# A hybrid mixer with a hierarchical mixture of experts: state products issued together, level differences on VectorE, gates through SBUF, weights staged in two buffers

## The chip, the cores and the metric

The kernel runs on one core of one Trainium2 chip. The metric is the device time of one execution in microseconds (us). The engines are TensorE (PE in the profile, with PEld for its weight loads), VectorE (DVE), ScalarE (ACT), GpSimd (POOL) and SyncE (SP), which issues most DMAs. Each engine works through its own instructions in the order in which they were put into its queue.

## What is computed

The input has 1024 tokens of width 1024. The reference, cut to what matters here:

```python
hq, hf, hi, hg, gq, gk, gv, ga, gg = jnp.split(x @ w_in, split_at, axis=-1)
f = lb + (1 - lb) * sigmoid(hf)
o_h = chunk_gla(hq * 128 ** -0.5, 1 - f, hi, log(f))           # 4 heads, key width 128
o_h = head_rms_norm(o_h, norm_h) * silu(hg)
log_a = log_sigmoid(ga @ w_a2 + b_a) / 16
o_g = chunk_gla(gq * 64 ** -0.5, gk, gv, log_a)                # 4 heads, key width 64
o_g = head_rms_norm(o_g, norm_g) * silu(gg)
h = concatenate([o_h, o_g]) @ w_out
x = layer_norm(ALPHA * x + h)
y = top-2 of 64 experts: (silu(x @ w_gate[e]) * (x @ w_up[e])) @ w_down[e], weighted
out = layer_norm(ALPHA * x + y)

# chunk_gla: with b the running sum of log_g inside a chunk,
#   o[t] = sum over s <= t of (q[t] * exp(b[t] - b[s]) . k[s]) v[s]  +  (q[t] * exp(b[t])) . S
#   S    = g_chunk * S + (k * exp(b_last - b))^T v                  (from chunk to chunk)
```

## The kernel before, in words

The kernel has three stages: the mixer (projections and gated linear attention), the output projection with the first norm and the router, and the experts.

**Projections.** `queue` (lines 265 to 279) is a list of 26 blocks of 128 columns of `w_in`: keys `k0..k5`, queries `q0..q5`, values `v0..v7`, gates `g0..g7`, and the low-rank input `ga`. `block(i)` (line 158) multiplies one such block with all tokens, in two halves of 512 tokens, each 24 matmuls of 128x512 (line 168) into one of two PSUM tiles `pp`; products are made of a rounded part and a rest (`wh` and `wl`, `xh` and `xl`). At its start a block has the next block's weights staged by `weights` (line 142): for each half of the weights SP loads the raw numbers into `wr` (line 154), ScalarE casts them into `wh` (line 155), and VectorE subtracts to get `wl` (line 156). After the last matmul of a half, the block's `evac` takes the result out of `pp`: keys and queries on ScalarE (lines 241 to 246); values by a copy into a tile `vt` (line 208), which TensorE later transposes (line 213) and VectorE copies into `VOA` (line 214); a gate by Silu on ScalarE (line 220) and a multiply into `VOA` on VectorE (line 222).

**Attention.** The loop `for u in range(6)` (line 625) goes through six units: four with one head of key width 128 and two with two heads of width 64. A unit's chunk is 128 tokens, so there are eight chunks. `prepare(u)` forms the log decays `lg` and their running sum `P` (lines 402 to 425). `level(li)` (line 459), for li from 0 to 6, scales keys and queries for the score blocks of size 2^li. For li from 1 on it forms a tile `d`: GpSimd subtracts `P` from a reference position for the first half of each block (line 481), ScalarE takes the exponential (line 482), VectorE multiplies the keys (line 483); GpSimd subtracts again for the second half (line 484), ScalarE takes the exponential (line 485), and VectorE multiplies the queries (line 486). Two buffers of `d` exist. `scores(li)` multiplies keys and queries on TensorE (line 497 and following) and VectorE masks the results into `acc` (lines 448 and 451). `states()` (line 561) multiplies the decayed keys `KLt` with the values for seven chunks (line 566), into two PSUM tiles of one bank each (four chunks and three), and VectorE chains the results: a copy for the first chunk (line 568), then one multiply-add per chunk (line 570) that reads the state before it. `outputs(half)` multiplies states and scores with queries and values (lines 583 and 586), ScalarE sums squares (line 591) and VectorE copies the result into `osb` (line 592). `norm()` (line 594) forms the inverse root of the mean square with thirteen small VectorE steps (lines 82 to 90) and multiplies `osb` (line 600); `turn_o` transposes it back into `VOA` (lines 607 and 608).

**Order.** TensorE's order is written out by hand in `mixer()` (line 613): `fill(n)` issues the next n projection matmuls, and the pieces of attention stand between such fills. Around the states of unit u the order is: the rest of the block, the fourteen instructions of `states()`, `fill(38)`, `outputs(0)` with the first three levels of unit u + 1 issued after it, `fill(38)`, `outputs(1)`, `norm()`, `fill(12)`, and then unit u + 1 with `scores(0)`, levels 3 and 4, `decayed_k`, `fill(26)`, `scores(1)`, `scores(2)`, levels 5 and 6, `fill(26)`, `turn_o(0)` of unit u, and so on. The order on the other engines is made by a scheduler out of the program's order. Where two instructions touch the same PSUM bank of a tile and one of them writes, the later one waits for the earlier one.

**Afterwards.** The output projection (`w_out`, line 899) and the router follow; then the loop over 32 pairs of experts (line 1276), whose weights SP loads in units of 2 MB into eight buffers (`load_unit`, line 758), each load as soon as the buffer's last reader is done.

Of the kernel before, what the change touches and what calls it, by code (L numbers as in the profile page):

```python
# [10 lines left out]
F32 = mybir.dt.float32  # L11
# [10 lines left out]
NT = T // 128  # L22
# [35 lines left out]
def mixer_moe_kernel(ctx: ExitStack, tc: tile.TileContext, x_in, xT_in, wf_in, wv_in, wvg_in, wa2_in,  # L58
# [68 lines left out]

    zt = g2.tile([128, 512], F32, name="vt", bufs=4)[:, 0:256].bitcast(BF)
    V.memset(zt, 0.0)
# [12 lines left out]
    def weights(i, parts=2):  # L142

        if queue[i][0] is None:
            wts[i] = gahl, None
            return
        hi = wst.tile([128, KT, 128], F32R, name="wh")
        lo = wst.tile([128, KT, 128], F32R, name="wl")
        m = KT // parts
        wts[i] = hi, lo  # L150
        for j in range(parts):
            ks = slice(j * m, j * m + m)
            raw = wst.tile([128, m, 128], F32, name="wr", bufs=1)
            nc.sync.dma_start(raw, queue[i][0][:, ks])
            heads.append(S.copy(hi[:, ks], raw))
            V.tensor_tensor(lo[:, ks], raw, hi[:, ks], OP.subtract)  # L156
# [45 lines left out]
    def to_rows(h):  # L202

        def evac(ps, ts):
            if len(late) > 3:
                late.pop(0)[1]()
            vt = g2.tile([128, 512], F32, name="vt", bufs=4)
            S.copy(vt, ps)

            def turn():  # L210
                tp = bank4()
                for i in range(4):
                    PE.transpose(tp[:, i], vt[:, i * 128:(i + 1) * 128], ident)
                V.tensor_copy(VOA[:, ts.start // 128:ts.stop // 128, h], tp)
            late.append((count[0] + 6, turn))
        return evac

    def gated(h):
        def evac(ps, ts):
            S.activation(ps, ps, AF.Silu)  # L220
            o = VOA[:, ts.start // 128:ts.stop // 128, h]
            V.tensor_tensor(o, o, ps.rearrange("p (a b) -> p a b", b=128), OP.mult)  # L222
        return evac
# [209 lines left out]
    def gla(u):  # L433
# [25 lines left out]
        def level(li):  # L459
# [16 lines left out]
            else:  # L476
                nb = T // (2 * h)
                e = g2.tile([128, T], F32, name="d")
                ev = v4(e)
                ref = Pv[:, :, 0, h - 1:h].to_broadcast([128, nb, h])  # L480
                G.tensor_tensor(ev[:, :, 0], ref, Pv[:, :, 0], OP.subtract)  # L481
                S.activation(ev[:, :, 0], ev[:, :, 0], AF.Exp, scale=sc)
                V.tensor_tensor(Kv[:, :, 0], kv[:, :, 0], ev[:, :, 0], OP.mult)
                G.tensor_tensor(ev[:, :, 1], Pv[:, :, 1], ref, OP.subtract)
                S.activation(ev[:, :, 1], ev[:, :, 1], AF.Exp, scale=sc)
# [75 lines left out]
        def states():  # L561
            ups = [bank4() for _ in range(2)]
            for c in range(NT - 1):
                up = ups[c // 4][:, c % 4]
                for hh in range(nh):
                    PE.matmul(up[rows[hh]], dd["KLt"][:, c, rows[hh]], VOA[:, c, h0 + hh], start=True, stop=True)
                if c == 0:
                    V.tensor_copy(St[:, c], up)
# [24 lines left out]

        def norm():

            sq = ssq[0].rearrange("p h c -> p (h c)")
            V.tensor_scalar(sq, sq, 1.0 / 128, None, op0=OP.mult)
            rs = rstd_of(small, sq, nh * NT, "n").rearrange("p (h c) -> p h c", h=nh)
# [3 lines left out]
        def turn_o(hh):  # L602
            gain = cols[:, 10 + h0 + hh:11 + h0 + hh]
            for half in range(2):
                tp = bank4()
                for i in range(4):
# [3 lines left out]
        return SimpleNamespace(level=level, scores=scores, decayed_q=decayed_q, decayed_k=decayed_k, turn_k=turn_k,  # L610
                               states=states, outputs=outputs, norm=norm, turn_o=turn_o, nh=nh, v=f"v{h0 + nh - 1}")

    def mixer():
# [11 lines left out]
        for u in range(6):  # L625
# [3 lines left out]
            un.level(3)  # L629
            un.level(4)  # L630
            un.decayed_k()
            fill(26)
# [43 lines left out]
            old.outputs(1)  # L676
            old.norm()
        fill(34)
# [894 lines left out]
```

## Time and profile before

| what | us |
|---|---|
| median of 2 runs | 1596.03 (1595.31 to 1596.76) |
| profiled execution: its time | 1599.36 |
| profiled execution: its span | 1597.6 |
| TensorE busy | 1461.5 (91% of the span) |
| VectorE busy | 705.7 |
| ScalarE busy | 438.6 |
| GpSimd busy | 388.7 |
| DMA from HBM | 447.58 MB read |

The profile is of one execution. A row of its groups gives line, engine, operation, output and inputs, shapes and count, and after the bar the busy time, the mean of one instruction in ns, and the idle time of the engine just before them with what ended it. In the timeline, the bracket at a row's end is the idle time of the engine before that instruction and its releaser. In a table of windows each engine has its busy time and, in brackets, its instruction count; PEclk is the share of full clock that TensorE was granted. A matmul of 128x512 is shown with 0.39 us, but such matmuls overlap: at full clock one starts about every 0.227 us.

### The profile page before, as it was taken

How to read it: one execution, taken by the hardware profiler on the slowest of the kernel's cores; microseconds unless marked ns; L12 is line 12 of the kernel's file. 1: busy time of each engine (PE TensorE's matmuls, PEld its weight loads, DVE VectorE, ACT ScalarE, POOL GpSimd, SP SyncE). 2: the span in 40 equal slices, each digit the busy share in tenths (PEclk: the TensorE clock that was granted, in tenths of full speed). 3: DMA queues.
4: the chain of work that ended last, by engine and by line, in shares of the span. 5: the costliest groups of instructions: out<-in, count | busy, mean ns of one | idle time of the engine just before them, and what ended most of it. 6: DMA issues, size and time to landing. Idle time of an engine off the chain costs nothing. (4 is left out here: it accounts for less than half of the span.)

```text
span 1597.6 us, 23051 instructions
## 1 busy us (share of the span) xinstructions
PE 1461.5 (91%) x9411; PEld 815.6 (51%) x9411; DVE 705.7 (44%) x1632; ACT 438.6 (27%) x915; POOL 388.7 (24%) x275
## 2 busy tenths in 40 slices
PE   8978989979889999999999999899989999989997
PEld 6766768767678887434333334334333334333342
DVE  6648456272736378333433324323323422422433
ACT  6535445333633243221211211211111111111120
POOL 1434223050600222131312211311311311321212
PEclk9989999988989999999999999999999999999999
DMA  4101001100013834999999999999999999999995
GB/s 167 41 27 35 26 29 35 27 29 28 21 35 124 318 138 175 406 425 426 427 425 426 427 426 426 426 425 426 425 426 427 427 425 425 427 426 426 426 419 221
DMA packets 62606, 449.14 MB, mean 281 GB/s; under 512 B 12320, under 2 KB 20768, under 8 KB 36896
## 3 DMA queue, kind: packets, MB, share of 16 engines
q1 hardware_dynamic: 51184, 430.01, 64.8%
q0 software_dynamic: 9216, 12.61, 2.2%
q10 hardware_dynamic: 2096, 5.01, 0.8%
q8 instruction: 75, 1.23, 0.3%
q14 instruction: 35, 0.29, 0.1%
HBM read 447.58 MB, written 20.97 MB: 293 GB/s over the span
## 5 line engine op out<-in xcount | busy, mean ns | idle before, releaser
L1298 PE MATMUL gu<-w2u,VOA 128*64 128x512 f32 x992 | 340.9, 597 | 20.3 <-DMA w2u<-in_wg_dram 11.4
L1298 PE MATMUL gu<-w1u,VOA 128*64 128x512 f32 x1040 | 344.0, 597 | 15.5 <-DMA w1u<-in_wg_dram 14.2
L1298 PEld LDWEIGHTS gu<-w2u,VOA 128*64 128x64 f32 x992 | 101.9, 137 | 200.1 <-issue 155.9
L1133 ACT ACTIVATE VOA<-tp,cols 128x128 f32<-128x128 f32 x256 | 96.1, 456 | 334.7 <-PE tp L1130 334.4
L1298 PEld LDWEIGHTS gu<-w1u,VOA 128*64 128x64 f32 x1040 | 106.4, 137 | 146.8 <-issue 113.1
L168 PE MATMUL pp<-xh,wh 128*128 128x512 f32 x416 | 173.6, 417 | 7.7 <-DVE VOA L222 4.2
L1341 PE MATMUL yp<-w2u,hT 128*64 128x512 f32 x496 | 170.0, 598 | 11.0 <-DVE hT L1150 11.0
L1341 PE MATMUL yp<-w1u,hT 128*64 128x512 f32 x496 | 168.0, 598 | 11.8 <-DVE hT L1150 11.8
L1120 POOL DMA_INDIRECT out_dram<-VOA,oidx x32 | 32.4, 1011 | 582.1 <-DVE VOA L1180 561.4
L168 PE MATMUL pp<-xl,wh 128*128 128x512 f32 x416 | 172.7, 415 | 0.0
L168 PE MATMUL pp<-xh,wl 128*128 128x512 f32 x416 | 172.6, 415 | 0.0
L1244 DVE SCALAR_TENSOR_TENSOR VOA<-VOA,cp 128x512 f32<-128x512 f32 x62 | 41.6, 682 | 259.5 <-PE cp L1230 250.3
L1157 DVE SCALAR_TENSOR_TENSOR y<-yp,gcol,y 128x512 fp32r<-128x512 f32 x62 | 46.5, 751 | 227.6 <-ACT y L1156 227.4
L481 POOL TENSOR_TENSOR d<-P 128x512 f32<-128x512 f32 x36 | 60.4, 1678 | 181.8 <-DVE P L425 70.6
L168 PEld LDWEIGHTS pp<-xh,wh 128*128 128x128 f32 x416 | 83.8, 201 | 28.3 <-DVE VOA L222 5.3
L1156 ACT ACTIVATE y<-yp,gcol 128x512 fp32r<-128x512 f32 x62 | 42.5, 687 | 187.9 <-PE yp L1341 185.4
L168 PEld LDWEIGHTS pp<-xl,wh 128*128 128x128 f32 x416 | 83.9, 202 | 18.4 <-issue 0.3
L168 PEld LDWEIGHTS pp<-xh,wl 128*128 128x128 f32 x416 | 83.9, 202 | 18.2 <-DVE wl L156 0.2
L1341 PEld LDWEIGHTS yp<-w1u,hT 128*64 128x64 f32 x496 | 48.1, 136 | 76.9 <-issue 60.3
L1304 ACT ACTIVATE sg<-gu 128x512 f32<-128x512 f32 x32 | 19.1, 598 | 247.9 <-PE gu L1298 247.9
L1341 PEld LDWEIGHTS yp<-w2u,hT 128*64 128x64 f32 x496 | 51.1, 136 | 62.0 <-issue 44.2
L1230 PE MATMUL cp<-y,same 128*128 128x512 f32 x316 | 82.1, 405 | 0.0
(313 smaller groups left out, 2096.8 us busy)
## 6 DMA issues: line engine op xcount, KB each, us to landing
w1u<-in_wg_dram SPq DMA_DIRECT2D x30, 2048.0 KB, 26.7
w2u<-in_wg_dram SPq DMA_DIRECT2D x30, 2048.0 KB, 29.0
w2u<-in_wu_dram SPq DMA_DIRECT2D x30, 2048.0 KB, 30.0
w1u<-in_wd_dram SPq DMA_DIRECT2D x30, 2048.0 KB, 28.9
w1u<-in_wu_dram SPq DMA_DIRECT2D x29, 2048.0 KB, 29.3
w2u<-in_wd_dram SPq DMA_DIRECT2D x28, 2048.0 KB, 28.9
wr<-in_wf_dram SPq DMA_DIRECT2D x36, 256.0 KB, 2.7
w1u<-in_wg_dram SPq DMA_DIRECT2D x6, 1024.0 KB, 26.3
```

Of the source, the lines that this page charges most:

```text
L168: PE.matmul(ps, w[:, k], x_[:, k, ts], start=(k == 0 and j == 0), stop=(k == KT - 1 and j == len(terms) - 1))
L481: G.tensor_tensor(ev[:, :, 0], ref, Pv[:, :, 0], OP.subtract)
L1120: return G.indirect_dma_start(out=dst, out_offset=bass.IndirectOffsetOnAxis(ap=idx, axis=0), in_=src, in_offset=None, bounds_check=rows - ...
L1133: S.activation(xt[:, c], tp[:, i], AF.Identity, bias=cols[:, 42 + c:43 + c], scale=cols[:, 34 + c:35 + c])
L1156: S.mul(yh[:, ns], yps[n], gate_col)
L1157: V.scalar_tensor_tensor(yl[:, ns], yps[n], gate_col, yh[:, ns], op0=OP.mult, op1=OP.subtract)
L1230: PE.matmul(cps[n], m, ys[q][:, i, n * 512:(n + 1) * 512], start=(not part and j == 0 and i == 0), stop=(not part and j == len(ms) - 1 and ...
L1244: o = V.scalar_tensor_tensor(xg[:, ns], xg[:, ns], ALPHA, cps[n], op0=OP.mult, op1=OP.add)
L1298: PE.matmul(dst[64 * b:64 * b + 64], xt[:, c, 64 * b:64 * b + 64], utile[6 * p + u + b][:, c], start=(c == 0), stop=(c == KT - 1))
L1304: silu = S.activation(sg, gp, AF.Silu)
L1341: PE.matmul(yps[n][64 * b:64 * b + 64], hT[:, c, 64 * b:64 * b + 64], utile[6 * p + 4 + b][:, c, n * 512:(n + 1) * 512], start=(c == 0), s ...
```

## The change

Seven edits, in the order of the diff. The pool `vt` has three buffers instead of four, and `late` (value halves waiting to be transposed) holds one less before the oldest is turned. `wr` has two buffers instead of one. For the gates of heads 0 to 5, Silu writes into a `vt` tile in SBUF instead of back into `pp`, and the multiply reads that tile. A level forms both halves' differences with one VectorE instruction over 1024 columns (`P` minus reference) instead of two GpSimd instructions over 512, and the first half's exponential takes the opposite sign of scale. `states()` issues the products of all seven chunks and then the chain. `norm()` of a unit is called in the next unit after its level 4, and its first VectorE step is ordered behind that level's last multiply; the last unit's norm is called after the loop.

```diff
-    zt = g2.tile([128, 512], F32, name="vt", bufs=4)[:, 0:256].bitcast(BF)
+    zt = g2.tile([128, 512], F32, name="vt", bufs=3)[:, 0:256].bitcast(BF)
...
-            raw = wst.tile([128, m, 128], F32, name="wr", bufs=1)
+            raw = wst.tile([128, m, 128], F32, name="wr", bufs=2)
...
-            if len(late) > 3:
+            if len(late) > 2:
                 late.pop(0)[1]()
-            vt = g2.tile([128, 512], F32, name="vt", bufs=4)
+            vt = g2.tile([128, 512], F32, name="vt", bufs=3)
             S.copy(vt, ps)
...
     def gated(h):
         def evac(ps, ts):
-            S.activation(ps, ps, AF.Silu)
+            gt = g2.tile([128, 512], F32, name="vt", bufs=3) if h < 6 else ps
+            S.activation(gt, ps, AF.Silu)
             o = VOA[:, ts.start // 128:ts.stop // 128, h]
-            V.tensor_tensor(o, o, ps.rearrange("p (a b) -> p a b", b=128), OP.mult)
+            V.tensor_tensor(o, o, gt.rearrange("p (a b) -> p a b", b=128), OP.mult)
...
                 ev = v4(e)
-                ref = Pv[:, :, 0, h - 1:h].to_broadcast([128, nb, h])
-                G.tensor_tensor(ev[:, :, 0], ref, Pv[:, :, 0], OP.subtract)
-                S.activation(ev[:, :, 0], ev[:, :, 0], AF.Exp, scale=sc)
+                b4 = lambda a: a.rearrange("p (b h) -> p b h", h=2 * h)
+                V.tensor_tensor(b4(e), b4(P), Pv[:, :, 0, h - 1:h].to_broadcast([128, nb, 2 * h]), OP.subtract)
+                S.activation(ev[:, :, 0], ev[:, :, 0], AF.Exp, scale=-sc)
                 V.tensor_tensor(Kv[:, :, 0], kv[:, :, 0], ev[:, :, 0], OP.mult)
-                G.tensor_tensor(ev[:, :, 1], Pv[:, :, 1], ref, OP.subtract)
                 S.activation(ev[:, :, 1], ev[:, :, 1], AF.Exp, scale=sc)
...
                 for hh in range(nh):
                     PE.matmul(up[rows[hh]], dd["KLt"][:, c, rows[hh]], VOA[:, c, h0 + hh], start=True, stop=True)
+            for c in range(NT - 1):
+                up = ups[c // 4][:, c % 4]
                 if c == 0:
                     V.tensor_copy(St[:, c], up)
...
-        def norm():
+        def norm(behind=None):
 
             sq = ssq[0].rearrange("p h c -> p (h c)")
-            V.tensor_scalar(sq, sq, 1.0 / 128, None, op0=OP.mult)
+            first = V.tensor_scalar(sq, sq, 1.0 / 128, None, op0=OP.mult)
+            if behind:
+                order(first, behind, "the levels go first")
...
             un.level(3)
             un.level(4)
+            if old:
+                old.norm(un.made[4])
             un.decayed_k()
...
             old.outputs(1)
-            old.norm()
+        old.norm()
```

The change moves instructions or their waits at three places that matter below.

On TensorE, at the states of unit 0, where line 566 is a state product, `KLt` the decayed keys, `VOA` the values and `mb` a PSUM bank; before:

```order
510 L168 MATMUL pp<-xl,wh 128x512
511 L566 MATMUL mb<-VOA,KLt 128x128 [waits DVE_49,Activation_49]
512 L566 MATMUL mb<-VOA,KLt 128x128 [waits DVE_49] x3
513 L566 MATMUL mb<-VOA,KLt 128x128 [waits Activation_49]
514 L566 MATMUL mb<-VOA,KLt 128x128 [waits DVE_49] x2
515 L168 MATMUL pp<-xh,wl 128x512
```

and of the change:

```order
510 L168 MATMUL pp<-xl,wh 128x512
511 L566 MATMUL mb<-VOA,KLt 128x128 [waits DVE_49,Activation_49]
512 L566 MATMUL mb<-VOA,KLt 128x128 x3
513 L566 MATMUL mb<-VOA,KLt 128x128 [waits DVE_49,Activation_49]
514 L566 MATMUL mb<-VOA,KLt 128x128 x2
515 L168 MATMUL pp<-xh,wl 128x512
```

The products stand where they stood; five of the seven no longer wait for VectorE, and the first of each bank still does.

On VectorE, at the same place, the chain of states (568 and 570, in the change 570 and 572) among the first levels of unit 1 (`KQ`, `d`) and the rests of the weights (156); before:

```order
73 L474 TENSOR_TENSOR KQ_108<-k,d 128x512
74 L156 TENSOR_TENSOR wl<-wr,wh 128x512
75 L472 TENSOR_TENSOR KQ_109<-q,d 128x512
76 L473 TENSOR_TENSOR KQ_109<-q,d 128x512
77 L568 COPY St<-mb 128x128
78 L475 TENSOR_TENSOR KQ_108<-k,d 128x512
79 L570 SCALAR_TENSOR_TENSOR St<-St,gdec,mb 128x128
80 L483 TENSOR_TENSOR KQ_110<-k,d 128x256x2
81 L570 SCALAR_TENSOR_TENSOR St<-St,gdec,mb 128x128
82 L156 TENSOR_TENSOR wl<-wr,wh 128x512
83 L570 SCALAR_TENSOR_TENSOR St<-St,gdec,mb 128x128
84 L486 TENSOR_TENSOR KQ_110<-q,d 128x256x2
```

and of the change:

```order
74 L475 TENSOR_TENSOR KQ_108<-k,d 128x512
75 L156 TENSOR_TENSOR wl<-wr,wh 128x512
76 L473 TENSOR_TENSOR KQ_109<-q,d 128x512
77 L156 TENSOR_TENSOR wl<-wr,wh 128x512
78 L474 TENSOR_TENSOR KQ_109<-q,d 128x512
79 L570 COPY St<-mb 128x128
80 L476 TENSOR_TENSOR KQ_108<-k,d 128x512
81 L572 SCALAR_TENSOR_TENSOR St<-St,gdec,mb 128x128
82 L482 TENSOR_TENSOR d<-P 128x1024
83 L572 SCALAR_TENSOR_TENSOR St<-St,gdec,mb 128x128
84 L482 TENSOR_TENSOR d<-P 128x1024
85 L572 SCALAR_TENSOR_TENSOR St<-St,gdec,mb 128x128
```

The chain keeps its place and its neighbours; both rests of the next weights now stand ahead of it, and the two wide subtracts (482) stand inside it.

On ScalarE, at the start of unit 4, where 208 is the copy of a value half that TensorE transposes next, 482 and 485 (in the change 483 and 485) are the exponentials of a level, and 549 is that of the decayed keys; before:

```order
204 L208 COPY vt<-pp 128x512
205 L155 CAST wh<-wr 128x512
206 L482 ACTIVATE d<-d 128x256x2
207 L485 ACTIVATE d<-d 128x256x2
208 L549 ACTIVATE lg<-lg 128x1024
209 L482 ACTIVATE d<-d 128x128x4
210 L485 ACTIVATE d<-d 128x128x4
211 L208 COPY vt<-pp 128x512
```

and of the change:

```order
204 L208 COPY vt<-pp 128x512
205 L155 CAST wh<-wr 128x512 x2
206 L549 ACTIVATE lg<-lg 128x1024
207 L208 COPY vt<-pp 128x512
208 L483 ACTIVATE d<-d 128x256x2
209 L485 ACTIVATE d<-d 128x256x2
210 L483 ACTIVATE d<-d 128x128x4
211 L485 ACTIVATE d<-d 128x128x4
```

The second copy of a value half stood behind the exponentials of two levels and now stands ahead of them.

More of the change, by code (lines that the diff above doesn't have):

```diff
@@ L610, in gla @@
         return SimpleNamespace(level=level, scores=scores, decayed_q=decayed_q, decayed_k=decayed_k, turn_k=turn_k,
-                               states=states, outputs=outputs, norm=norm, turn_o=turn_o, nh=nh, v=f"v{h0 + nh - 1}")
+                               states=states, outputs=outputs, norm=norm, turn_o=turn_o, made=made, nh=nh, v=f"v{h0 + nh - 1}")
     def mixer():
```

## The prediction

> **What bounds the kernel now.** I read the slices of the page first, then a table of windows by stage, then what TensorE waits for, then windows around the waits. The slices split the run in two.
>
> ```profile
> PEclk9989999988989999999999999999999999999999
> DMA  4101001100013834999999999999999999999995
> ```
>
> From the sixteenth slice on (640 us) the DMA engines are busy all the time: the experts' weights stream, and nothing in this change touches them. Before that the DMA is nearly idle and the granted TensorE clock dips again and again. By stage (columns: window, its length, busy time and count of PE, PEld, DVE, ACT and POOL, granted clock, DMA share, GB/s):
>
> ```profile
> 12.00:516.00 504.00, 452.62 (x4867) 362.69 (x4866) 282.34 (x512) 229.60 (x466) 141.72 (x106) 0.92 0.13 40
> 516.00:640.00 124.00, 120.91 (x708) 100.57 (x706) 80.72 (x353) 38.21 (x77) 28.68 (x37) 1.00 0.55 214
> 640.00:1597.60 957.60, 880.64 (x3813) 347.72 (x3813) 338.78 (x762) 165.13 (x363) 216.12 (x126) 1.00 0.99 417
> ```
>
> The mixer (12 to 516) is TensorE's. It idles 504 - 452.6 = 51.4 us there and works at 0.92 of its clock: at full clock its work would take 452.6 x 0.92 = 416 us, so about 88 us are lost. From 516 to 640 it is busy 97% at full clock and starts when the mixer ends; the weights follow at 0.99. So whatever the mixer gains arrives at the end in full, unless the stream were limited by something that does not move; I see nothing of that kind. What TensorE waits for in the mixer (us in total, times, longest):
>
> ```profile
> PE mb L566 <- DVE St L570: 14.7, 24, 1.3
> PE mb L566 <- DVE St L568: 14.3, 6, 5.3
> PE mb L497 <- issue: 8.6, 4, 2.4
> PE mb L213 <- ACT vt L208: 5.8, 2, 5.2
> PE pp L168 <- DVE VOA L222: 4.2, 2, 2.6
> PE pp L168 <- ACT wh L155: 3.5, 1, 3.5
> ```
>
> These six make 51.1 of the 51.4 us. The first two, 29.0 us, are the state products (line 566) that wait for the chain on VectorE. Around the six units' states:
>
> ```profile
> 80.00:100.00 20.00, 11.99 (x38) 9.07 (x37) 12.69 (x17) 8.88 (x14) 12.42 (x9) 0.66 0.08 26
> 148.00:168.00 20.00, 12.01 (x43) 9.20 (x42) 14.80 (x24) 10.71 (x17) 12.75 (x9) 0.74 0.08 27
> 216.00:232.00 16.00, 10.40 (x40) 8.04 (x39) 9.65 (x22) 8.09 (x10) 5.05 (x3) 0.79 0.11 33
> 288.00:304.00 16.00, 13.62 (x50) 9.97 (x49) 4.52 (x11) 2.57 (x5) 0.00 (x0) 0.79 0.12 33
> 376.00:388.00 12.00, 9.38 (x46) 5.88 (x45) 4.54 (x11) 2.57 (x5) 0.00 (x0) 0.72 0.16 44
> 460.00:476.00 16.00, 13.58 (x66) 9.60 (x64) 5.04 (x11) 1.97 (x4) 0.00 (x0) 0.79 0.06 19
> ```
>
> The loss of a window is its length less PE busy times clock: 12.1, 11.1, 7.8, 5.2, 5.2 and 5.3, together **46.7 us**: 29.0 of idling and 17.7 of slow clock after it. The other waits, the same way:
>
> ```profile
> 48.00:60.00 12.00, 8.98 (x151) 7.21 (x152) 9.00 (x11) 5.71 (x9) 7.83 (x6) 0.72 0.07 23
> 324.00:340.00 16.00, 10.85 (x161) 8.51 (x161) 12.25 (x18) 9.05 (x21) 10.43 (x8) 0.79 0.11 34
> 340.00:352.00 12.00, 9.65 (x283) 7.73 (x282) 10.10 (x19) 3.11 (x6) 7.65 (x4) 0.86 0.08 26
> 356.00:364.00 8.00, 5.62 (x156) 4.62 (x145) 3.37 (x8) 2.81 (x6) 1.58 (x4) 0.79 0.02 4
> 424.00:440.00 16.00, 11.46 (x282) 8.76 (x281) 15.05 (x34) 8.24 (x14) 9.77 (x4) 0.79 0.09 30
> 440.00:452.00 12.00, 10.02 (x287) 8.38 (x286) 7.24 (x17) 4.93 (x9) 1.58 (x4) 0.86 0.13 38
> ```
>
> They lose 5.5, 7.4, 3.7, 3.6, 6.9 and 3.4, together 30.5 us.
>
> **The change part by part.**
>
> *State products in front.* Unit 0 before, on TensorE:
>
> ```profile
> 79.70 0.39 PE L168 MATMUL pp<-xh,wh 128*128 128x512 f32 x1
> 79.92 0.40 PE L168 MATMUL pp<-xl,wh 128*128 128x512 f32 x1
> 80.16 0.38 PE L566 MATMUL mb<-VOA,KLt 128*128 128x128 f32 x2
> 85.87 0.80 PE L566 MATMUL mb<-VOA,KLt 128*128 128x128 f32 x2 [5.33 <-DVE St L568]
> 87.11 0.80 PE L566 MATMUL mb<-VOA,KLt 128*128 128x128 f32 x2 [0.44 <-DVE St L570]
> ```
>
> and on VectorE:
>
> ```profile
> 82.64 2.38 DVE L472 TENSOR_TENSOR KQ<-q,d 128x512 f32<-128x512 f32 x1
> 84.94 0.68 DVE L473 TENSOR_TENSOR KQ<-q,d 128x512 f32<-128x512 f32 x1
> 85.54 0.28 DVE L568 COPY St<-mb 128x128 f32<-128x128 f32 x1
> ```
>
> The second product shares its bank with the first, whose result VectorE fetches 5.4 us later (85.54 - 80.16), because older work stands ahead in its queue; then every product makes a round trip. In the change five of seven products wait for nothing, and TensorE goes straight into its 38 matmuls, 0.23 us apart (79.70 to 79.92): 8.7 us of cover, and the chain is needed only behind them, by `outputs(0)`, which reads the first three states. Is it ready? By the order, VectorE needs at most 5.4 us plus one more weight rest (0.68, from line 473, the same shape) to line 568; then three chain steps of about 0.3 (line 568), one multiply of 0.68 and one wide subtract of 1.22 (below) give 8.9 us. TensorE needs 8.7 plus some 1.6 for its 14 products (the pair at 80.16): the chain is about 1.4 us early, more if the 2.38 us of line 472, a shape that takes 0.68 in the next row, shrinks with GpSimd's work gone. If that cover were gone, each unit would lose the lateness itself. Bounds: 29.0 (the clock is not regained) to 46.7; I take **42**, near the upper end since the chain is covered.
>
> *Weights in two buffers.* In 48:60 TensorE waits 3.5 us for a cast, which waits on a load that could not start before the one buffer was free, and sits in ScalarE's queue behind exponentials that wait for GpSimd. With two buffers both loads go out together. Bounds 0 to 5.5; I take **4**.
>
> *ScalarE's order at unit 4.* In 324:340 TensorE waits 5.2 us for the copy of line 208, which stood behind four exponentials; now it stands ahead of them. Bounds 0 to 7.4; I take **5**.
>
> *Gates through SBUF.* TensorE waits twice (4.2 us) until the multiply of line 222 has read `pp`; now `pp` is free after Silu. The second wait lies in 424:440, whose loss of 6.9 also holds one bank wait of about 2. Bounds 0 to 1.6 + 4.9 = 6.5; I take **5**. The smaller pool `vt` costs nothing: never more than two value halves wait at once.
>
> *Differences on VectorE.* Removed, added, and what a unit has room for (rows of groups, of one line's durations, and a window over unit 0's states to unit 1's):
>
> ```profile
> L481 POOL TENSOR_TENSOR d<-P 128x512 f32<-128x512 f32 x36 | 60.4, 1678 | 181.8 <-DVE P L425 70.6 <-DVE ny L86 42.5 <-DVE nt L88 27.1
> ...
> L600 DVE TENSOR_TENSOR osb<-osb,ny 128x1024 f32<-128x1024 f32 x8 | 9.6, 1219 | 0.1
> ```
>
> ```profile
> L483 DVE TENSOR_TENSOR KQ<-k,d x36: 678/686/2371, 40.8 to 438.3; 128x512 f32<-128x512 f32 x36
> ```
>
> ```profile
> 80.16:150.74 70.58, 62.57 (x638) 51.53 (x637) 40.72 (x72) 29.69 (x61) 21.39 (x18) 0.90 0.10 31
> ```
>
> The 36 wide subtracts are not in the trace. Line 600 has their operation, type, size and a broadcast operand: 1.22 us. From below, 0.68 (half the columns); from above, twice the slowest half, 2 x 2.371 = 4.74. I take 1.22: 44 us in all, 7.3 per unit. VectorE is busy 40.7 of a unit's 70.6 us; with 7.3 more it is 48.0, while TensorE's own work is 62.57 x 0.90 = 56.3. It stays below, and work such as line 483, from 0.68 to 2.37 us, should come to its lower end. So it hides behind TensorE; the bank waits of line 497 (8.6 us idle, losses 3.7, 3.6, 3.4 and about 2 = 12.7), where masks come late on VectorE, may shrink a little. Bounds -3 to 12.7; I take **3**.
>
> *Norm behind level 4.* Thirteen small steps at 0.28 (the nearest row, line 568) and 1.22 are 4.8 us. They used to run right after `outputs(1)`; now `turn_o(0)`, 52 matmuls (12 us) and two score groups later, is closer behind them, and TensorE would wait for it with all its matmuls queued behind. VectorE has about as much to do there as the time holds, so units 1 to 5 may lose about 1 us each. Bounds 0 to 12 lost; I take **-4**.
>
> Sum: 42 + 4 + 5 + 5 + 3 - 4 = **55 us**. The profiled execution took 1599.36 us (span 1597.6); 1599.4 - 55 = 1544.4, and the median lies 3.3 below that execution: **1541 us**.
>
> **The clock.** That a slow stretch follows such waits is in the rows, but not how long a wait must be:
>
> ```profile
> 468.09 0.70 PE L566 MATMUL mb<-VOA,KLt 128*64 128x128 f32 x4 [0.45 <-DVE St L570]
> 468.71 0.79 PE L168 MATMUL pp<-xl,wh 128*128 128x512 f32 x1
> 469.31 0.63 PE L168 MATMUL pp<-xh,wl 128*128 128x512 f32 x1
> 469.73 0.63 PE L168 MATMUL pp<-xh,wh 128*128 128x512 f32 x1
> ```
>
> Unit 5 idles only 16 - 13.58 = 2.4 us, in pieces of at most 1.3, and yet its next matmuls are 0.42 us apart. The Trainium skill, "TensorE: Matmul & The Clock Gate", section "Why this matters for your kernels", speaks of gaps over about 3 us, one idle window, before the clock halves. By that rule the low clock of units 3 to 5 would not come from these waits and would stay; the rows, with the dip behind each of the six, speak for the waits, and I sum by the rows.
>
> **The rivals.**
>
> *The clock stays low in units 3 to 5.* For it: their idle pieces are short. Against it: the dips stand at the states and nowhere near by. Their losses are 15.7, of which idling is 2.38 + 2.62 + 2.42 = 7.4, so 8.3 us fewer gained: 1549.
>
> *VectorE's queue gives the gain back at `turn_o`.* If the whole norm, 4.8 us, comes late in each of five units, TensorE idles 24 us, and at the states' ratio of loss to idling (46.7 / 29.0 = 1.6) loses 38 instead of 4: 1541 + 34 = 1575. For it: VectorE is in order and 48 of 56 us full. Against it: it runs without GpSimd's interference.
>
> *The bank waits go too.* With masks in time, all 12.7 and the full bounds of the other terms, with 4 lost to the norm: 46.7 + 5.5 + 7.4 + 6.5 + 12.7 - 4 = 74.8, so 1521.
>
> *Slower: VectorE becomes the bound.* If the wide subtract, whose broadcast blocks are as short as four columns, takes 4.74 us, a unit's VectorE work is 40.7 + 6 x 4.74 = 69.2, and about 8 us of waiting for ScalarE and TensorE in order make 77 against 70.6 now: six units lose 6 x 3.4 to 6 x 6.4; with 3.4, because the interference leaves, 1596 + 20 = 1616. It decides from about 4.1 us a subtract on. Against it: line 483 reads the same short blocks in 0.68.
>
> That the change does not do what it says is excluded by the order of its instructions: the products' waits are gone.
>
> **How the numbers follow.** Chances: forecast 0.62 (its own range 1526 to 1558), bank waits gone too 0.12, clock stays low 0.06, norm late 0.15, slower 0.05. The range leaves out most of the slower case and half of the late norm: 1520 to 1570. Two per cent of 1596, about what a measurement of this kernel tells from no change, are 32 us, so the line is 1564. Faster: 0.62 + 0.12 + 0.06 and a third of 0.15: 0.85. Same: the rest of that case and half of the slower one: 0.13. Slower: 0.02.
>
> **What would show it.** Right: line 566 without idle time behind line 568 or 570, a granted clock near 1.00 behind each of the six states, the experts' stream starting some 55 us earlier, the wide subtract at 1.22 us, POOL's busy time down by over 100 us. Wrong: a new wait of `outputs(0)` for the chain (lines 585 and 588 of the change), long waits of the transposes behind the norm, VectorE close to full, or a mixer that gained while the end did not move.

## The result and the profile after

The changed kernel takes 1533.88 us (median of 2 runs, 1532.65 to 1535.10) against 1596.03 before: a ratio of 0.9611 with a 95% interval of 0.9569 to 0.9652, so some 62 us less. Five more runs of the same kernel, later and on another chip, gave 1532.25 (1531.06 to 1533.09), 0.9583 [0.9570, 0.9596]. The forecast was 1541 in a range of 1520 to 1570. The profiled execution took 1535.10 us (span 1533.3), 64.3 less than the profiled one of before.

By stage, as before (window, its length, busy time and count of PE, PEld, DVE, ACT and POOL, granted clock, DMA share, GB/s):

```profile
12.00:452.00 440.00, 422.56 (x4867) 345.98 (x4867) 275.94 (x540) 227.85 (x470) 42.43 (x34) 0.98 0.15 46
452.00:576.00 124.00, 120.84 (x708) 100.55 (x707) 81.35 (x360) 38.29 (x77) 29.00 (x37) 1.00 0.55 214
576.00:1533.30 957.30, 878.76 (x3813) 348.58 (x3813) 337.10 (x762) 165.44 (x363) 216.23 (x126) 1.00 0.99 417
```

The mixer is 64 us shorter (504 to 440), and the two stages behind it are as long as they were (124 and 957.3 against 957.6). The whole gain is the mixer's and arrives at the end in full. TensorE idles 440 - 422.56 = 17.4 us there, 51.4 before, and its clock is 0.98 where it was 0.92. What it still waits for (us in total, times, longest):

```profile
PE mb L497 <- issue: 8.5, 4, 2.4
PE mb L213 <- ACT vt L208: 4.2, 2, 2.7
PE mb L611 <- DVE osb L604: 3.7, 3, 2.5
PE pp L168 <- DVE wl L156: 0.9, 1, 0.9
```

The state products' 29.0 us are gone, and so are the waits for the gates' multiply and for the weights' cast. The 8.6 us of line 497 are still there, to a tenth. Lines 611 and 604 are the output transposes and the norm's last step (607 and 600 before); that wait is new. Unit 0's states after, on TensorE:

```profile
74.82 1.72 PE L566 MATMUL mb<-VOA,KLt 128*128 128x128 f32 x14
76.30 0.48 PE L168 MATMUL pp<-xh,wl 128*128 128x512 f32 x1
...
85.71 0.39 PE L585 MATMUL mb<-St,QI 128*128 128x128 f32 x2
```

and the first and third step of their chain on VectorE:

```profile
79.44 0.28 DVE L570 COPY St<-mb 128x128 f32<-128x128 f32 x1
...
81.64 0.34 DVE L572 SCALAR_TENSOR_TENSOR St<-St,gdec,mb 128x128 f32<-128x128 f32 x1
```

All 14 product instructions pass in 1.5 us. The third state is there at 82.0 (81.64 + 0.34), and the outputs want it from 85.71 on: 3.7 us of slack, where the forecast had 1.4. In the window over this place TensorE is busy without a break at full clock:

```profile
72.00:92.00 20.00, 20.00 (x106) 17.04 (x105) 17.28 (x30) 12.88 (x29) 1.90 (x1) 1.00 0.09 27
```

Behind the state products of units 3 to 5, which start at 251.56, 328.05 and 404.81, it is the same; four us of each:

```profile
256.00:260.00 4.00, 4.00 (x19) 3.29 (x19) 0.57 (x2) 0.34 (x1) 0.00 (x0) 1.00 0.06 24
332.00:336.00 4.00, 4.00 (x20) 3.30 (x19) 1.05 (x4) 0.00 (x0) 0.00 (x0) 1.00 0.13 47
408.00:412.00 4.00, 4.00 (x23) 3.31 (x21) 2.40 (x6) 0.70 (x2) 0.00 (x0) 1.00 0.42 119
```

The two large costs that were not in the trace of before, as minimum, median and maximum in ns:

```profile
L482 DVE TENSOR_TENSOR d<-P x36: 1215/1222/1270, 36.7 to 376.0; 128x1024 f32<-128x1024 f32 x36
```

```profile
L484 DVE TENSOR_TENSOR KQ<-k,d x36: 681/687/699, 42.9 to 379.1; 128x512 f32<-128x512 f32 x36
```

The wide subtract is 1.22 us, as taken from line 600, whatever the length of its blocks. The multiply of line 484 (483 before) has lost its slow cases: its longest is 0.70 us, 2.37 before. GpSimd's busy time fell by 98.9 us (388.7 to 289.8), just short of the 100 that the forecast named as a sign, because the subtract that stayed there (line 547) grew from 13.1 to 24.7 us.

### The profile page after: what moved, and what is told of

It reads as the page before. It is cut to its first block, busy times and chain, and to the rows that moved or that the text cites. A ratio compares the mean times of both kernels' runs of the same rounds, so it can differ in the third digit from the quotient of the medians.

```text
span 1533.3 us, 22993 instructions
## 1 busy us (share of the span) xinstructions
PE 1429.6 (93%) x9411; PEld 799.8 (52%) x9411; DVE 698.3 (46%) x1668; ACT 437.2 (29%) x919; POOL 289.8 (19%) x203
## 5 line engine op out<-in xcount | busy, mean ns | idle before, releaser
L1304 PE MATMUL gu<-w2u,VOA 128*64 128x512 f32 x992 | 340.8, 597 | 21.1 <-DMA w2u<-in_wg_dram 11.1
L168 PE MATMUL pp<-xh,wl 128*128 128x512 f32 x416 | 166.0, 399 | 0.9 <-DVE wl L156 0.9
L168 PE MATMUL pp<-xl,wh 128*128 128x512 f32 x416 | 166.5, 400 | 0.0
L168 PE MATMUL pp<-xh,wh 128*128 128x512 f32 x416 | 165.8, 399 | 0.0
L168 PEld LDWEIGHTS pp<-xh,wl 128*128 128x128 f32 x416 | 79.7, 192 | 17.7 <-DVE wl L156 1.4
L168 PEld LDWEIGHTS pp<-xh,wh 128*128 128x128 f32 x416 | 79.8, 192 | 17.5 <-issue 0.7
L168 PEld LDWEIGHTS pp<-xl,wh 128*128 128x128 f32 x416 | 79.4, 191 | 16.8 <-issue 0.2
L1206 POOL TENSOR_TENSOR VOA<-VOA 128x1024 f32<-128x1024 f32 x32 | 77.7, 2429 | 2.5
```

The lines of the kernel that those rows point to most:

```text
L168: PE.matmul(ps, w[:, k], x_[:, k, ts], start=(k == 0 and j == 0), stop=(k == KT - 1 and j == len(terms) - 1))
L1206: E.tensor_tensor(o, o, ln1[1], OP.add)
L1304: PE.matmul(dst[64 * b:64 * b + 64], xt[:, c, 64 * b:64 * b + 64], utile[6 * p + u + b][:, c], start=(c == 0), stop=(c == KT - 1))
```

## The experiments

All medians stand beside runs of the kernel before on the same chip (1596.65 to 1598.63); the changed kernel is at 1532 to 1534. It ran beside only two of the others, so gains and losses against it are given from both of its medians.

| kernel | median, us | ratio to before, 95% |
|---|---|---|
| states alone on the kernel before | 1555.76 | 0.9731 [0.9713, 0.9749] |
| changed, states undone | 1584.47 | 0.9907 [0.9887, 0.9927] |
| level differences alone on the kernel before | 1583.36 | 0.9900 [0.9870, 0.9931] |
| changed, norm back | 1526.67 | 0.9553 [0.9534, 0.9572] |
| changed, one weight buffer | 1536.81 | 0.9627 [0.9611, 0.9643] |
| changed, Silu in PSUM | 1531.14 | 0.9587 [0.9571, 0.9603] |
| changed, score products spread | 1528.31 | 0.9567 [0.9549, 0.9585] |
| changed, decayed keys on VectorE | 1525.27 | 0.9549 [0.9533, 0.9565] |
| states and level differences alone on before | 1530.69 | 0.9576 [0.9563, 0.9590] |
| changed, once more | 1532.25 | 0.9583 [0.9570, 0.9596] |
| changed, four edits together | 1515.70 | 0.9480 [0.9466, 0.9493] |
| the same, spread wider | 1513.71 | 0.9470 [0.9454, 0.9487] |

### The state products, alone and taken out

On the kernel before, the one edit:

```diff
                 for hh in range(nh):
                     PE.matmul(up[rows[hh]], dd["KLt"][:, c, rows[hh]], VOA[:, c, h0 + hh], start=True, stop=True)
+            for c in range(NT - 1):
+                up = ups[c // 4][:, c % 4]
                 if c == 0:
```

> The kernel before with one edit: the state products stand in front of their chain; all else as before. Theory (the 29.0 us of idling at the states and the 17.7 us of low clock behind them are one loss, and both go): 42 to 47 us less than 1596, so 1549 to 1554, no wait of the states' products for VectorE and a clock near 1.00 behind all six groups. Rival 1 (the chain needs the other edits, since VectorE's multiplies are still slowed by GpSimd): the outputs wait for the chain, and only 20 to 35 us are gained, 1561 to 1576. Rival 2 (the low clock does not come from these short waits): 29 us and no more in idling, clock still about 0.8 in units 3 to 5, 1558 to 1567.

1555.76 us, 43 less than the 1598.63 beside it: within the theory's 42 to 47, 2 us above its absolute number. No wait for the chain is left, so rival 1 falls. Behind the states of units 3 to 5 TensorE is busy without a break at a clock of 1.00 (16 us each, from 268, 345 and 425), so rival 2 falls too. But something else came late. TensorE's waits, in a profiled execution of 1561.28 us, the longest of the four (the others take 1555.65 to 1555.77):

```profile
PE mb L213 <- ACT vt L208: 16.9, 5, 5.2
PE mb L497 <- issue: 8.1, 4, 2.4
PE pp L168 <- DVE VOA L222: 4.2, 2, 2.7
PE pp L168 <- ACT wh L155: 3.5, 1, 3.5
```

The state waits have gone, and the value copies of line 208 on ScalarE have grown from 5.8 to 16.9 us. In unit 0, where the outputs should follow the states, TensorE stands still for 4.67 us:

```profile
87.74 0.39 PE L168 MATMUL pp<-xh,wh 128*128 128x512 f32 x1
92.80 1.12 PE L213 MATMUL mb<-cst,vt 128*128 128x128 f32 x4 [4.67 <-ACT vt L208]
```

ScalarE meanwhile:

```profile
86.73 0.64 ACT L482 ACTIVATE d<-d 128x512 f32<-128x512 f32 x1 [1.81 <-POOL d L481]
87.28 0.60 ACT L155 CAST wh<-wr 128x512 fp32r<-128x512 f32 x1
88.42 0.63 ACT L485 ACTIVATE d<-d 128x512 f32<-128x512 f32 x1 [0.54 <-POOL d L484]
90.09 0.63 ACT L482 ACTIVATE d<-d 128x512 f32<-128x512 f32 x1 [1.04 <-POOL d L481]
91.64 0.63 ACT L485 ACTIVATE d<-d 128x512 f32<-128x512 f32 x1 [0.92 <-POOL d L484]
92.17 0.57 ACT L208 COPY vt<-pp 128x512 f32<-128x512 f32 x1
```

The copy stands behind four exponentials, and each of them waits for a difference from GpSimd. Before, the states' own waits covered this: TensorE was late anyway. So in this execution a stall of 29.0 us was removed, and 11.1 us went to the next one in line.

The other way round, the changed kernel with these lines taken out again:

> The changed kernel with the state products back between the steps of their chain; all other edits stay. Theory (the terms add up): the other edits are worth the rest of the 62 us, 15 to 20, so 1576 to 1581. Rival (VectorE, without GpSimd beside it, reaches the chain's first step earlier, so that the first wait of 14.3 us in six units shrinks by itself to 5 or less, and the terms overlap): 1560 to 1570.

1584.47 us, 51 to 52 more than the changed kernel and 14 less than the kernel before: a little below the theory's 15 to 20, and far from the rival's 1560 to 1570. TensorE waits 16.2 us for line 570 and 10.7 us for line 568, where before it was 14.7 and 14.3: the first wait shrank by 3.6 us only, so the rival's overlap is small. The edit is worth 43 us by itself and 51 in the company of the others.

### The level differences alone

On the kernel before, the level differences as the changed kernel has them, and nothing else:

```diff
-                G.tensor_tensor(ev[:, :, 0], ref, Pv[:, :, 0], OP.subtract)
-                S.activation(ev[:, :, 0], ev[:, :, 0], AF.Exp, scale=sc)
+                V.tensor_tensor(b4(e), b4(P), Pv[:, :, 0, h - 1:h].to_broadcast([128, nb, 2 * h]), OP.subtract)
+                S.activation(ev[:, :, 0], ev[:, :, 0], AF.Exp, scale=-sc)
...
-                G.tensor_tensor(ev[:, :, 1], Pv[:, :, 1], ref, OP.subtract)
```

> The kernel before with the level differences on VectorE in one step for both halves, and nothing else changed. Theory (the waits of 8.6 us at the score products are not waits for masks, and TensorE's instructions run dry there; the edit moves the end only through earlier work of VectorE at the states): 0 to 8 us less, 1588 to 1596, and the score products' waits still about 8.5 us. Rival (contention between GpSimd and VectorE is what the change lives on): 15 us or more less, 1581 or below. Third (VectorE too full): slower than 1600.

1583.36 us, 15 less than before (ratio 0.9870 to 0.9931, so 11 to 21 us): nearer to the rival than to the theory. The theory's half on line 497 (496 here) holds, its half on the gain does not:

```profile
PE mb L565 <- DVE St L569: 16.2, 24, 1.8
PE mb L565 <- DVE St L567: 11.7, 6, 4.0
PE mb L496 <- issue: 8.7, 4, 2.4
PE mb L213 <- ACT vt L208: 2.7, 1, 2.7
...
PE pp L168 <- ACT wh L155: 1.2, 1, 1.2
PE pp L168 <- DVE VOA L222: 0.3, 1, 0.3
```

With one buffer and Silu in PSUM, as before, the wait for the cast falls from 3.5 to 1.2 us, that for the gates' multiply from 4.2 to 0.3, and that for the value copy from 5.8 to 2.7. These are the three waits for which the forecast credited three other edits. Two things became faster here at once. ScalarE's exponentials of the levels waited 76.4 us for GpSimd before (55.0 and 21.4) and wait 27.5 for VectorE now. And VectorE's own multiplies of lines 483 and 486 take 49.7 us in place of 66.9. No run separates the two.

### Those two edits together

> The kernel before with two of the change's edits: the state products in front of their chain, and the level differences on VectorE. One staging buffer, Silu in PSUM with four value buffers, and the norm at the end of its loop stay as before. Theory (these two carry the whole gain; taken one by one out of the changed kernel, the later norm cost 7, Silu through SBUF 2 to 3, and the second buffer brought some 3): 1534 - 7 - 3 + 3 = 1527, so 1524 to 1530, and no wait over 1.5 us for the gates' multiply or for a cast. Rival (the waits for the gates' multiply of 4.2 us and for the cast of 3.5 us come back as soon as the state products stop hiding them, as the prediction priced them): 1538 to 1545.

1530.69 us: the state products and the level differences carry the whole gain, against 1532.25 for the full change on the same chip; the intervals lie on each other. The theory had the mechanism right and the time 0.7 us too low (its range ended at 1530). On top of the states alone the differences are worth 25 us (1555.76 to 1530.69), since the value copies then come in time (3.7 us of waits in all where the states alone left 16.9). The waits for the gates' multiply are gone altogether, and that for a cast is 0.9 us. The rival, the forecast's own pricing, falls. The repeat beside it:

> The changed kernel once more, on the chip of the two kernels beside it. Both theories: 1531 to 1537.

1532.25 us, as expected.

### The other edits, one by one out of the changed kernel

The norm back at the end of its loop:

```diff
-            if old:
-                old.norm(un.made[4])
...
             old.outputs(1)
-        old.norm()
+            old.norm()
```

> The changed kernel with the norm of a head back at the end of its loop, directly behind the second half of the outputs and ahead of the next unit's levels 3 and 4 on VectorE. Theory (the three waits of 3.7 us at the transposes of line 611, with the slow clock behind them, are the price of the later norm): 4 to 6 us less than the changed kernel, 1528 to 1530. Rival (the norm in front holds up the levels, and the score products of levels 3 and 4 or the value copies wait in its stead): the same or up to 8 us more, 1534 to 1542.

1526.67 us (1525.87 to 1528.29), 5.6 to 7.2 less, all four runs below every run of the changed kernel: the theory, with a little more than it had. The wait of line 611 falls from 3.7 to 0.2 us, that of line 497 from 8.5 to 7.3, and the others stay within 0.5. Why the later norm is late can be seen on VectorE in unit 5 of the changed kernel:

```profile
370.81 0.17 DVE L599 TENSOR_SCALAR ssq<-ssq 128x16 f32<-128x16 f32 x1
370.88 1.22 DVE L552 TENSOR_TENSOR lg<-k,lg 128x1024 f32<-128x1024 f32 x1
372.02 0.17 DVE L82 TENSOR_SCALAR nve<-ssq 128x16 f32<-128x16 f32 x1
...
379.72 2.37 DVE L604 TENSOR_TENSOR osb<-osb,ny 128x1024 f32<-128x1024 f32 x2
```

```profile
381.10 1.94 PE L611 MATMUL mb<-cst,osb 128*128 128x128 f32 x8 [2.46 <-DVE osb L604]
```

The small steps are cheap, 0.17 us, but in the queue each is followed by an instruction of the next unit, so that the norm lasts from 370.81 to 382.1, 11.3 us where the forecast added its steps up to 4.8. With the norm back, its steps alternate with other work too: it lasts 8.9 us, from 362.75 to 371.6 in its kernel, and the transposes of line 611 start at 374.67 without a wait. There it begins as soon as the copies into `osb` (line 594) are done; in the changed kernel these end at 367.8, and the norm begins 3.0 us later. So the move costs a later start of 3.0 us and 2.4 us of longer alternation.

One staging buffer (`bufs=2` to `bufs=1`):

> The changed kernel with one staging buffer for the weights in place of two. Theory (the wait of 3.5 us for a cast at 48 to 60 us comes back, with its slow clock): 4 to 6 us more than 1534, so 1538 to 1540, and a wait of line 168 for line 155 of some 3 us. Rival (ScalarE's queue was the cause of that wait and has been cleared by the difference on VectorE): within 1 us of 1534.

1536.81 us (1535.18 to 1538.56), 3 to 5 more, with a wait of line 168 for line 155 of 1.0 us, not 3: its mechanism is not the theory's. The 3.5 us of before were mostly the queue on ScalarE, as the rival had it, though the time is not within its 1 us. Where the 3 to 5 us go stays open: the profiled execution is the fastest of the four (1535.18 us), and TensorE's waits in it add up to about what they are in the changed kernel.

Silu back into PSUM (`gt = ps`):

> The changed kernel with Silu writing back into PSUM and the multiply reading there, so that a projection bank is free only after the multiply on VectorE. Theory (the two waits of line 168 for the gate's multiply, 4.2 us before, come back): 4 to 7 us more, 1538 to 1541. Rival (VectorE is no longer late there, since GpSimd leaves its multiplies at 0.68 us): within 1 us of 1534, and no such wait over 0.5 us.

1531.14 us (1530.30 to 1531.24): no loss, and no wait for the multiply at all. The rival's reason holds, and the time is 1 to 3 us less, not the same: the SBUF detour brings nothing once the differences have left GpSimd. That the waits of line 611 are 2.4 us there, not 3.7, fits this, but the ratios cannot be told apart.

### What is left: line 497

The forecast called the waits of line 497 bank waits. Where they stand, in unit 4 of the changed kernel:

```profile
306.75 2.26 PE L497 MATMUL mb<-KQ 64*32 64x16 f32 x242
311.29 0.28 PE L497 MATMUL mb<-KQ 64*32 64x16 f32 x14 [2.27 <-issue]
```

A pair of score groups is 256 rows, 128 to a group, and every group writes both its banks from its first chunk on. The stall comes after 242 of them, in the middle of the second group, where no bank and no operand is new. (The other three come after 149, 250 and 215.) So the edit was to leave the banks as they are and thin out the products:

```diff
                 for c in range(NT):
+                    if nh == 2 and li in (2, 4) and c in (2, 4, 6):
+                        fill(3)
                     for hh in range(nh):
...
-            fill(26)
+            fill(26 if un.nh == 1 else 17)
```

> The changed kernel; in the two units with two heads, nine projection products are put in threes into the second score group of each pair, and as many fewer follow it. No bank is taken or freed in another order: the group's first product stands where it stood. Theory (TensorE's instructions run dry after some 215 to 242 tiny products of about 9 ns each, in the middle of a group): the waits of 8.5 us at line 497 fall below 2 us, and the end comes 8 to 12 us earlier, 1522 to 1526. Rival (the products wait for a bank that the masks on VectorE have not yet given free, as the prediction had it): the waits stand at the group's first product and stay, within 2 us of 1534.

1528.31 us (1525.63 to 1530.03), 4 to 6 less, and line 497's waits (499 there) fall from 8.5 to 2.0. The pair above, now:

```profile
307.31 1.55 PE L499 MATMUL mb<-KQ 64*32 64x16 f32 x160
309.69 0.34 PE L499 MATMUL mb<-KQ 64*32 64x16 f32 x32
```

This fits the theory: TensorE works these off at about 9.7 ns each (1.45 us for 150 of them in a later kernel) with a weight load to each, and its instructions do not arrive at that rate. The trace has signs of their arrival. Each of the four pauses in the changed kernel ends 2.3 to 2.7 us after a packet of the DMA queue that the profile calls "instruction"; here the one ahead of the pause that ends at 311.29, in slices of 0.1 us from 308:

```profile
DMA  0000070000000000000000000000000000000000
q8 instruction: 1, 0.02, 1.9%
```

And it is the place that counts, more than the number. In all kernels that do not spread the products the pauses come after 148 to 152, 242 to 246, 249 to 254 and 215 to 219 of them, though all else around them moved; three runs have one more short pause after 114 or 115. This reads as products that come to the end of what has arrived and wait for the next packet. That a given number of them in a row runs the supply dry is not shown. The gain is about half of what was expected; the wait of line 611 for the late norm grew from 3.7 to 4.9.

### What is left: line 208

In unit 4 the value copy still holds TensorE for 2.7 us. ScalarE at that place in the changed kernel:

```profile
280.44 1.06 ACT L549 ACTIVATE lg<-lg 128x1024 f32<-128x1024 f32 x1 [6.95 <-POOL lg L547]
281.40 0.57 ACT L208 COPY vt<-pp 128x512 f32<-128x512 f32 x1
```

The copy stands behind an exponential, and this waits for the large subtract that is left on GpSimd in every unit, that of the decayed keys:

```profile
L547 POOL TENSOR_TENSOR lg<-P x6: 1894/4203/6274, 34.5 to 351.2; 128x1024 f32<-128x1024 f32 x6
```

The change itself made this worse: before, the six took 13.1 us and ScalarE waited 7.2 us for them; in the changed kernel, where VectorE's wide subtracts run beside some of them, they take 24.7 and ScalarE waits 21.8.

The edit gives it to VectorE (`G.tensor_tensor` to `V.tensor_tensor` in line 547).

> The changed kernel with the subtract of the decayed keys (line 547), the last large one on GpSimd, on VectorE. Theory (on GpSimd it takes 1.9 to 6.3 us because VectorE works beside it, ScalarE waits 21.8 us for it, and in unit 4 the copy of the values stands behind it): about 1.2 us on VectorE, the waits of line 213 for the copy of line 208 fall from 4.2 to below 2 us, 3 to 5 us less, 1529 to 1531. Rival (VectorE's queue is full at that place, and 1.2 us more holds up level 4 and the norm): the wait of line 611 for the norm grows by 3 us or more, and the time is 1534 to 1542.

1525.27 us (1524.16 to 1525.62), 7 to 9 less, more than the theory's 3 to 5. The subtract now takes 1.22 us:

```profile
L547 DVE TENSOR_TENSOR lg<-P x6: 1218/1226/1231, 47.0 to 356.1; 128x1024 f32<-128x1024 f32 x6
```

ScalarE's wait for it falls from 21.8 to 4.1 us, the value copies' from 4.2 to 1.5, and the norm's, against the rival, from 3.7 to 1.3: VectorE has 7.3 us of subtracts more (its busy time grows by 2.0) and is earlier all the same, since it itself waits less for ScalarE's exponentials (line 484: 0.9 us, 11.3 in the changed kernel).

### All of it together

> The changed kernel with the norm back at the end of its loop, Silu back in PSUM, the tiny score products spread by threes of projection products, and the subtract of the decayed keys on VectorE. Theory (one by one they gained 7.2, 2.7, 5.6 and 8.6, 24.1 together; the first and the last both relieve the waits of line 611, up to 4 us twice counted): 1510 to 1516. Rival (the last one's gain was the clearing of VectorE's place that the norm wants, and the extra 7 us of VectorE fall on the levels once the norm stands in front of them): 1518 to 1524, with waits of score products for VectorE.

1515.70 us (1513.84 to 1516.75), in the theory's interval: 82 us below the kernel before, 17 below the changed kernel. Of the waits, 2.8 us of line 497 (499 there), 1.2 of the value copy and 0.2 of the norm are left. Of the 2.8, 2.5 are one stall after 150 products, ahead of the first place where anything was put between. So, last:

```diff
-                    if nh == 2 and li in (2, 4) and c in (2, 4, 6):
-                        fill(3)
+                    if nh == 2 and li and c % 2 == 0 and (c or li % 2 == 0):
+                        fill(2)
...
-            fill(26 if un.nh == 1 else 17)
+            fill(26 if un.nh == 1 else 12)
```

> The last kernel (the four edits on the changed kernel) with the projection products put in by twos, and into both score groups of a pair in the units with two heads, so that no more than 32 tiny products stand together where 160 did; as many fewer follow the pair. Theory (TensorE's instructions still run dry in unit 4, 2.5 us after the first 150 of them, and the clock is low for some 10 us behind it, 7.2 us lost from 280 to 300 us with a value copy's wait of 1.2): the waits at line 499 are gone, below 0.5 us, and the time is 4 to 6 us less than 1515.7, so 1510 to 1512. Rival (supply runs dry at that place whatever is put between, since it is the number of instructions and not their rate): the wait of 2.5 us stays, 1514 to 1517.

1513.71 us (1512.91 to 1514.87). The waits of line 499 are gone, so the rival's mechanism falls. The time lies between the two forecasts: the gain is 2 us where 4 to 6 were expected, and the intervals overlap. In the mixer TensorE now idles 1.4 us in 428, at full clock:

```profile
12.00:440.00 428.00, 426.62 (x4906) 343.65 (x4905) 282.88 (x563) 233.01 (x476) 19.43 (x30) 1.00 0.17 56
```

Part of the difference is the price of the alternation itself:

```profile
284.61 0.34 PE L499 MATMUL mb<-KQ 64*32 64x16 f32 x32
284.88 0.50 PE L168 MATMUL pp<-xh,wh 128*128 128x512 f32 x1
...
285.54 0.34 PE L499 MATMUL mb<-KQ 64*32 64x16 f32 x32
```

One round takes 0.93 us (284.61 to 285.54); 32 products at 9.7 ns and two matmuls at 0.227 would be 0.76. There are 28 such insertions where the kernel above had 12, so about 16 x 0.17 = 2.7 us go there, an estimate from this round. The rest is within what these runs resolve.

## Why the prediction was right, and where its reasons were not

**The bound** held: the mixer is TensorE's, and what it gained reached the end, 64.0 us of 64.3 between the profiled executions.

**State products in front**, 42: right in mechanism and size. Taken alone it measured 43, and 51 beside the other edits. The chain was covered, with 3.7 us to spare in unit 0, and the slow stretches behind all six states went with the waits. What the forecast did not see is that the wait also covered a late value copy on ScalarE, which takes back 11 us of waiting if the differences stay on GpSimd.

**Differences on VectorE**, 3: the mis-sized term. Price and place of the subtract were right (1.22 us, hidden), but the step "it hides behind TensorE; the bank waits of line 497 may shrink a little" looked only at VectorE. What it left out is ScalarE: its exponentials no longer wait for GpSimd, and all that stands behind them comes earlier. It measured 15 us alone and 25 on top of the state products. How much of this came through VectorE's own shorter multiplies, which the forecast did name, is not separated.

**Weights 4, ScalarE's order 5, gates 5**: their waits shrank (for the cast 3.5 to 0, with a new one of 0.9 for the rest of the weights; 5.8 to 4.2; 4.2 to 0), but mostly through the differences. One buffer costs 3 to 5 us, so the 4 came true as a number, though not by the wait that it was meant for; Silu through SBUF brings nothing, and the value copy of unit 4 is still 2.7 us late, held by the subtract that stayed on GpSimd. The forecast had the cause in hand, exponentials that wait for GpSimd in ScalarE's queue, and gave the cure to the second buffer.

**Norm**, -4: right in sign, and the norm's move costs 5.6 to 7.2. The sum of its steps, 4.8 us, was not what lasted: interleaved, it took 11.3, and it began 3.0 us later.

**Line 497**: "bank waits" was wrong, and it did no harm because the term was small. They fit pauses in the supply of instructions: thinning out the products ended them, packets of the instruction queue stand ahead of them, and the change left them as they were.

So the sum, 55 us, came out at 62 to 66, with two errors against each other: 12 to 22 us too little for the differences, and some 10 too much for the edits whose waits the differences remove anyway (14 credited; 3 to 5 found for the buffer, none for Silu, and ScalarE's order was not run alone). That the sum came out near is in part luck.

**The rivals.** Behind the states of units 3 to 5 no dip is left, so the first rival falls: the dips there followed waits of 0.39 to 0.68 us, five in each unit and one close behind another (the forecast's 1.3 is the longest of all six units). The Trainium skill, "TensorE: Matmul & The Clock Gate", section "Why this matters for your kernels", speaks of gaps over some 3 us; by that alone these dips would have stayed, and the traces disagree. The late norm is real, at a fifth of the price that the rival set on it, or less. The waits of line 497 stayed. VectorE is not the bound: its busy time fell from 705.7 to 698.3 us although it took over 44 us of subtracts.

## What to carry to other kernels

When an in-order engine waits for a slow one, price the work behind it in its queue, not only the wait itself: here moving 36 pairs of subtracts off GpSimd was worth 15 to 25 us, much of it through the copies and casts that stood behind ScalarE's exponentials. Before a stall is credited to one edit, ask which wait ends second there; taking each edit alone and taking it out of the whole gave both answers in two runs. And a chain of short dependent steps costs its place in the queue, not the sum of its steps.

## What the runs showed of the hardware

**Short waits add up for the clock.** In unit 3 of the kernel before, five waits of 0.39 to 0.67 us, from 291.3 to 295.8, go with a clock of 0.79 over 288 to 304. In the kernel with the states alone, one wait of 1.58 us (before line 168 at 385.55) left the next window at full clock:

```profile
384.00:388.00 4.00, 2.45 (x11) 2.00 (x12) 2.19 (x4) 3.96 (x9) 2.11 (x2) 1.00 0.02 4
388.00:392.00 4.00, 4.00 (x256) 3.41 (x255) 2.62 (x10) 3.98 (x18) 0.00 (x0) 1.00 0.22 70
```

In the changed kernel waits of 1.47 and 1.57 us, 3.6 us apart (ends at 292.59 and 296.17), cost half the clock in the window behind them:

```profile
292.00:296.00 4.00, 2.02 (x153) 1.75 (x153) 4.00 (x11) 1.06 (x3) 0.00 (x0) 0.95 0.01 4
296.00:300.00 4.00, 3.83 (x113) 3.30 (x114) 4.00 (x16) 1.15 (x2) 0.00 (x0) 0.50 0.52 137
```

A longer wait does it alone. Behind the 2.27 us before line 497 at 311.29, 13 us after the end of the wait before it, the next window has 0.59:

```profile
312.00:316.00 4.00, 4.00 (x12) 3.13 (x12) 1.03 (x3) 3.35 (x7) 1.53 (x4) 0.59 0.02 4
```

The tiny products around the last two cases are not the reason: 160 of them without a pause (at 307.31, products spread) leave the clock at 1.00 from 304 to 316. These are one instance of each; how long a stretch the clock looks at was not tried.

**TensorE can run out of instructions.** Where 256 products of 9 to 10 ns stand in a row, pauses of 1.4 to 2.5 us come at the same places of the order in every kernel; with 32 in a row and two longer matmuls between, in the last kernel, there are none. Each of the four pauses in the changed kernel ends 2.3 to 2.7 us after a packet of the instruction queue. That queue moves 38 packets in the mixer (0.62 MB, so 16 KB each), and only these four go with such a pause. What decides when a packet is fetched was not tried.

**GpSimd and VectorE slow each other both ways.** The same 128x1024 subtract is 1.22 us on VectorE and 1.9 to 6.3 on GpSimd; VectorE's multiplies of line 483 go up to 2.37 us beside GpSimd and, as line 484 of the changed kernel, to 0.70 without its subtracts. In the kernel before, GpSimd's 128x512 subtract takes 1.04 us where VectorE is idle (line 481 at 47.70) and 5.37 where it is busy (at 429.29). This fits the Trainium skill, "SBUF — State Buffer", section "Who interferes with whom": a VectorE instruction with two SBUF inputs contends with a GpSimd one that reads SBUF.
